# Streamed operand blocks 2080 instead of 2048 bytes apart in a two-layer decoder trunk

## The chip, the cores and the metric

The kernel runs on one core of a Trainium2 chip. The metric is the device time of one execution in microseconds. Three runs of the kernel before gave 2125.79, 2126.0 and 2127.0 us, median 2126.0 us. Nothing else runs on the chip.

## The reference

The program is a decoder trunk of two layers over 256 positions with a model width of 2048, all in float32. What matters here is its large products; everything else is small beside them.

```python
D_MODEL = 2048; SEQ = 256; DEPTH = 2; D_FF = 5632
# layer 0: chunked gMLP gating (12 groups x 128) beside 4-head cross-attention into 256 memory tokens
z = h @ w_in_a[l]                                   # 2048 x 3584
# layer 1: latent attention (12 heads) beside the same cross-attention
kv = rmsnorm(x, g_kv) @ w_kv_a;  z = h @ w_in_b[j]  # 2048 x 576, 2048 x 1024
...
kv = rmsnorm(mem, g_mem) @ w_mem_kv                 # 2048 x 1024, each layer
x = x + jnp.concatenate([main, mo], axis=-1) @ w_out[l]               # 2048 x 2048, each layer
x = x + conv_ffn(rmsnorm(x, g_ffn[l]), w_ffn_up[l], ..., w_ffn_down[l])  # 2048 x 11264, 5632 x 2048
```

The output is a final RMSNorm of x, 256 x 2048.

## The kernel before, in words

**Operands.** TensorE multiplies in the format float32r, which keeps fewer bits than float32, so every large product is made of three: high part by high part, low part by high part, high part by low part. An activation operand is a tile of 16 blocks; block k holds the 128 features k*128 to k*128+127 on the partitions, and along the partition 256 positions of the high part and then 256 of the low part, 512 columns or 2048 bytes in all. There are four such big operands: `xhl` (the normalized stream), `memhl` (the memory tokens), `mainhl` (what w_out multiplies) and `h` (the hidden units of the ffn). The last three share one place in SBUF (tag "big"); `xhl` has its own (tag "xhl"), and in layer B the plain tile `scratch` takes that place. The smaller operands `qhl` and `chl` of layer B have the same 2048-byte blocks, in a pool of their own.

**Weights.** `chunk` (L92 to L125) loads two k-blocks of 512 columns, 512 KB, by one DMA from SP's queue into `raw` (L98), ScalarE rounds them into `whi` (L117), and VectorE writes the remainder to `wlo` (L118; with a gain L122 and L123). Each of the three has four buffers of 4096 bytes on a partition, and `schedule_with_timeline_sim` lets a planner set the order of the instructions on each engine.

**Feature-major products.** `gemm_fm` (L158) takes two chunks at a time, that is four k-blocks by up to four output blocks. Inside a chunk the loop goes over output blocks, and innermost over the two k-blocks, so consecutive matmuls stream block k, block k+1, block k, block k+1 and so on of the same pair. `mm_fm` (L135) makes two bursts of them: `high` (L140) streams all 512 columns of a block against `whi`, `low` (L144) streams the first 256 against `wlo` and adds into the second half of the accumulator. The two bursts change places from one pair of chunks to the next, so that two bursts of one kind follow each other. Each matmul has its own load of a 128 x 128 weight block (LDWEIGHTS, shown as PEld).

**Token-major products.** `gemm_tm` (L187) turns the roles round: `mm_tm` (L179) streams 512 columns of `whi` (L182), `wlo` (L183) and `whi` again (L184), and the weight that is loaded into the array is a 128-column piece of the operand. It serves the values of the memory attention, the first projection of layer A, the values of layer B and the down-projection of the second ffn.

**Writers of the operands.** `put_mem` (L436) writes two blocks of `memhl` by one ScalarE and one VectorE instruction; `split` and `split_gain` (L227 to L235) write one block at a time. `new_hl` (L532) makes a new `xhl` tile for each product that writes one, and `ffn` (L558) one `h` tile for each of its three parts.

The weights of a chunk begin at multiples of 512 bytes within the 4096-byte buffers, and the blocks of the operands at multiples of 2048 bytes within their tiles.

Of the kernel before, what the change touches and what calls it, by code (L numbers as in the profile page):

```python
# [8 lines left out]
F32 = mybir.dt.float32  # L9
F32R = mybir.dt.float32r  # L10
# [3 lines left out]
ALU = mybir.AluOpType  # L14
AX = mybir.AxisListType

P = 128
D = 2048
S = 256
NB = D // P  # L20
# [10 lines left out]
THETA = 10000.0  # L31
EPS = 1e-6
FF_GROUPS = (4, 4, 3)


def exact_pieces(value, bits, count):
# [30 lines left out]
    return out  # L67


class Kernel:  # L70
    def __init__(self, ctx, tc, t, out):
        self.tc, self.nc, self.t, self.out = tc, tc.nc, t, out
# [11 lines left out]

    def psum(self, dt=F32):
        return self.ps.tile([P, 512], dt, tag="ps", name=self.uid("ps"))

    def tmp(self, pool, shape, tag, bufs=2, dt=F32):
        return pool.tile(shape, dt, tag=tag, name=self.uid(tag), bufs=bufs)
# [330 lines left out]
    def start(self):  # L420
        nc, t, tc = self.nc, self.t, self.tc
        self.x = self.ap.tile([P, NB, S], F32, name="xT")
        self.xhl = self.ap.tile([P, NB, 512], F32R, tag="xhl", name=self.uid("xhl"))
        mhl = self.ap.tile([P, NB, 512], F32R, tag="big", name=self.uid("memhl"))
        self.kT = [pool.tile([P, MH, S], F32, name=self.uid("kT")) for pool in (self.mk, self.cp)]
        self.mv = [pool.tile([P, 2, MW], F32, name=self.uid("mv")) for pool in (self.mk, self.cp)]
        self.rt = self.cp.tile([P, 2], F32, name="rt0")
        self.rb = self.tmp(self.cp, [P, S], "rbc", 2)
        with tc.tile_pool(name="st", bufs=1) as st:
            self.gp = st  # L430
            mtok = [st.tile([P, D], F32, name=f"mtok{tb}") for tb in range(2)]
            xtok = [st.tile([P, D], F32, name=f"xtok{tb}") for tb in range(2)]
            mrt = st.tile([P, 2], F32, name="mrt")
            mrb = st.tile([P, S], F32, name="mrb")

            def put_mem(k, acc):  # L436
                a = acc.rearrange("p (k s) -> p k s", k=2)
                hi = mhl[:, k : k + 2, :S]
                nc.scalar.activation(hi, a, AF.Copy)
                nc.vector.tensor_tensor(mhl[:, k : k + 2, S:], a, hi.bitcast(F32), ALU.subtract)  # L440

            def put_x(k, acc):
                for i in range(2):
                    self.split_gain(self.xhl[:, k + i, :], acc[:, i * S : (i + 1) * S], self.gain("g_mix", k + i))
                nc.scalar.activation(self.x[:, k : k + 2, :], acc.rearrange("p (k s) -> p k s", k=2), AF.Copy)

            def mem_piece(h):
                return lambda: (self.token_load(t["mem"][0], mtok, h), self.token_transpose(mtok, h, put_mem))

            load = lambda h: lambda: self.token_load(t["x"][0], xtok, h)  # L450
            trans = lambda h: lambda: self.token_transpose(xtok, h, put_x)
            self.token_load(t["mem"][0], mtok, 0)
            self.gains(("g_mem",))
            self.token_transpose(mtok, 0, put_mem)
            hooks = [
                {
                    0: [mem_piece(1)], 2: [mem_piece(2)], 4: [mem_piece(3)],
                    5: [lambda: self.token_rstd(mtok, st, mrt), lambda: self.gains(("g_mix", "g_ffn", "g_kv"))],
                    6: [self.masks],
                    7: [lambda: self.spread(mrb, mrt)],  # L460
                },
                {
                    0: [load(0), load(1)], 1: [load(2), load(3)], 3: [trans(0)], 5: [trans(1)],
                    6: [lambda: self.gains(("g_v", "g_kv_lat", "g_q_lat"))],
                },
                {0: [trans(2)], 2: [trans(3)], 4: [lambda: self.token_rstd(xtok, st, self.rt)]},
                {1: [lambda: self.spread(self.rb, self.rt)], 2: [lambda: self.conv_consts(0)], 4: [lambda: self.conv_consts(1)]},
            ]
            for l in range(2):
                w = t["w_mem_kv"][l]  # L470
                kT, v = self.kT[l], self.mv[l]

                def ek(b, acc):
                    nc.gpsimd.tensor_tensor(kT[:, b, :], self.join(acc), mrb, ALU.mult)

                def ev(tb, acc):
                    nc.scalar.activation(v[:, tb, :], acc, AF.Copy, scale=mrt[:, tb : tb + 1])

                m = lambda k: mhl[:, k, :]
                g = lambda k: self.gain("g_mem", l * NB + k)  # L480
                self.gemm_fm(self.rows(w, 0, MW), list(range(NB)), MH, m, ek, gain=g, hooks=hooks[2 * l])
                self.gemm_tm(self.rows(w, MW, MW), NB, MW, m, ev, gain=g, hooks=hooks[2 * l + 1])
# [47 lines left out]
        nc.vector.tensor_tensor(x[:, j, :], acc[:, S:], x[:, j, :], ALU.add)  # L530

    def new_hl(self):  # L532
        self.xhl = self.ap.tile([P, NB, 512], F32R, tag="xhl", name=self.uid("xhl"))
        self.ssum = self.tmp(self.cp, [P, S], "ssum", 2)

    def next_operand(self, j, gain):
# [21 lines left out]
    def ffn(self, l, after=None, to_tokens=None, tokens=None):  # L558
        nc, t = self.nc, self.t
        rb = self.tmp(self.cp, [P, S], "rbc", 2)  # L560
        xhl, ssum = self.xhl, self.ssum
        first = {1: [lambda: self.rstd_bc(rb, ssum, D)]}
        up, down = t["w_ffn_up"][l], t["w_ffn_down"][l]
        with self.tc.tile_pool(name=self.uid("ff"), bufs=1) as fp:
            g0 = 0
            for part, ng in enumerate(FF_GROUPS):
                h = self.ap.tile([P, NB, 512], F32R, tag="big", name=self.uid("h"))

                def conv(b, acc):
                    a = self.tmp(fp, [P, S], "a", 2)  # L570
                    nc.gpsimd.tensor_tensor(a, self.join(acc), rb, ALU.mult)  # L571
                    c = self.tmp(fp, [P, S], "c", 3)
                    w = lambda j: self.cT[:, l, j, b : b + 1]
                    nc.scalar.activation(c, a, AF.Identity, scale=w(2), bias=w(3))  # L574
                    nc.vector.scalar_tensor_tensor(c[:, 1:], a[:, : S - 1], w(1), c[:, 1:], ALU.mult, ALU.add)  # L575
                    nc.vector.scalar_tensor_tensor(c[:, 2:], a[:, : S - 2], w(0), c[:, 2:], ALU.mult, ALU.add)  # L576
                    return c

                for g in range(g0, g0 + ng):
                    gate = self.tmp(fp, [P, 4, S], "gate", 2)  # L580

                    def eg(b, acc):
                        c = conv(4 * g + b, acc)
                        nc.scalar.activation(gate[:, b, :], c, AF.Silu)

                    def ev(b, acc):
                        c = conv(FB + 4 * g + b, acc)
                        hv = self.tmp(fp, [P, S], "hv", 2)
                        nc.vector.tensor_tensor(hv, gate[:, b, :], c, ALU.mult)
                        self.split(h[:, 4 * (g - g0) + b, :], hv)  # L590

                    ks = list(range(NB))
                    turns = to_tokens if to_tokens is not None and g == 1 else {}
                    self.gemm_fm(self.rows(up, g * 512, 512), ks, 4, lambda k: xhl[:, k, :], eg, hooks=first if g == 0 else {})
                    self.gemm_fm(self.rows(up, FF + g * 512, 512), ks, 4, lambda k: xhl[:, k, :], ev, hooks=turns)
                last = part == len(FF_GROUPS) - 1
                if last and l == 0:
                    self.new_hl()
                dn = down[g0 * 512 : (g0 + ng) * 512]
                for j in range(4):  # L600
                    src = self.rows(dn, j * 512, 512)
                    if tokens is not None:
                        self.gemm_tm(
                            src, 4 * ng, 512, lambda k: h[:, k, :], lambda tb, acc: tokens(j, tb, acc, last), late=3 if last and j == 3 else 0
                        )
                        continue

                    def ed(b, acc):
                        self.add_residual(4 * j + b, acc)
                        if last:  # L610
                            after(4 * j + b)

                    self.gemm_fm(src, list(range(4 * ng)), 4, lambda k: h[:, k, :], ed)
                g0 += ng


    def layer_a(self):
        nc, t, tc = self.nc, self.t, self.tc
# [3 lines left out]
        with ExitStack() as ctx:  # L622
# [51 lines left out]
            hooks = {1: [spatial_weights], **{4 + i: [lambda i=i: gates(3 * i)] for i in range(4)}}  # L674
            self.gemm_fm(self.rows(w, 2 * GW, MW), ks, MH, x, eq, hooks=hooks)

            hl = self.ap.tile([P, NB, 512], F32R, tag="big", name=self.uid("mainhl"))
            p = {}

            def scores(h):  # L680
# [31 lines left out]
    def layer_b(self):  # L712
# [9 lines left out]
        with tc.tile_pool(name="lb", bufs=1) as lb:  # L722
# [49 lines left out]
            hooks = {2: [lambda: rotate(krT, kr)], 5: [lambda: fq(qhl, QR, "g_q_lat")]}  # L772
            self.gemm_fm(self.rows(w, QR, MW), ks, MH, x, em, gain=gm, hooks=hooks)

            hl = self.ap.tile([P, NB, 512], F32R, tag="big", name=self.uid("mainhl"))
            scratch = self.ap.tile([P, NB * 512], F32, tag="xhl", name="scratch")
            v = scratch[:, : 2 * GW].rearrange("p (a c) -> p a c", a=2)
            wuv = t["w_uv"][0].rearrange("r h v -> r (h v)")

# [221 lines left out]
```

## Time and profile before

| | before |
|---|---|
| median of three runs | 2126.0 us |
| span of the profiled execution, first to last instruction | 2125.1 us |
| PE busy | 2101.5 us, 99% of the span |
| PEld busy | 1831.1 us, 86% |
| VectorE busy | 1465.7 us, 69% |
| ScalarE busy | 1148.7 us, 54% |
| GpSimd busy | 392.8 us, 18% |
| mean granted TensorE clock | 0.998 |
| moved from and to HBM | 392.01 MB, 184 GB/s over the span |

The span leaves out what lies around the first and last instruction, which is why the runs, at 2125.79 us and up, stand a little above it. A busy time of PE counts a matmul from its start to its modelled end, and consecutive matmuls overlap: a burst is best read from the start of its first matmul to the start of what follows, divided by the number of matmuls. That quotient is called the pace below.

### The profile page before, as it was taken

To read this page: it belongs to the slowest core of one execution; us is meant where nothing else is said; L and a number is where in the kernel's file an instruction comes from. 1 tells how busy PE (TensorE), PEld (TensorE's weight loads), DVE (VectorE), ACT (ScalarE), POOL (GpSimd) and SP (SyncE) were. 2 spreads that over 40 slices of the span, in tenths; PEclk is the share of its full clock that TensorE was granted. 3 is DMA by queue.
4 is the path that set the end of the run, shared out by engine and by line. 5 is a ranking of instruction groups with operands and counts; after the bars stand their busy time and mean duration, and the time that the engine had idled before them with its cause. 6 is when DMAs were issued, how large, how long until landed. Compare 5 with 4: busy or idle time off the path is not lost.

```text
span 2125.1 us, 31077 instructions
## 1 busy us (share of the span) xinstructions
PE 2101.5 (99%) x11624; PEld 1831.1 (86%) x11624; DVE 1465.7 (69%) x2186; ACT 1148.7 (54%) x1773; POOL 392.8 (18%) x378
## 2 busy tenths in 40 slices
PE   8999999999999999999999999999999999999998
PEld 7888888888888888888888788888888888888886
DVE  6655667777756777567798766677775577745775
ACT  7654654556535555356556554466553555535554
POOL 1000123312101121011254111332120121201210
PEclk9999999999999999999999999999999999999999
DMA  8565555666566665666655533665656666656664
GB/s 272 178 202 178 159 187 189 189 189 191 189 194 187 185 195 188 197 182 188 192 181 165 171 114 110 196 190 170 191 196 195 187 190 190 194 195 188 189 188 149
DMA packets 207548, 392.01 MB, mean 184 GB/s; under 512 B 14302, under 2 KB 22820, under 8 KB 207268
## 3 DMA queue, kind: packets, MB, share of 16 engines
q1 hardware_dynamic: 207252, 389.50, 59.3%
q8 instruction: 91, 1.49, 0.3%
q14 instruction: 61, 0.50, 0.1%
q10 hardware_dynamic: 144, 0.52, 0.1%
HBM read 387.88 MB, written 2.10 MB: 184 GB/s over the span
## 4 chain that ended last, share of the span: by engine, by line
PE 97%; DVE 1%; ACT 1%; DMA 1%; issue 0%; SPq 0%; DVEq 0%; ACTq 0%
PE ps L140 50%; PE ps L144 26%; PE ps L182 6%; PE ps L184 6%; PE ps L183 6%; PE ps L831 1%; DMA raw<-in_w_mem_kv 0%; PE ps L829 0%; PE ps L523 0%; PE ps L488 0%; DVE wlo L118 0%; PE ps L665 0%; PE ps L852 0%; DMA raw<-in_w_in_a 0%; PE ps L393 0%
## 5 line engine op out<-in xcount | busy, mean ns | idle before, releaser
L118 DVE TENSOR_TENSOR wlo<-raw,whi 128x1024 fp32r<-128x1024 f32 x660 | 843.1, 1288 | 490.3 <-ACT whi L117 362.4
L117 ACT ACTIVATE whi<-raw 128x1024 fp32r<-128x1024 f32 x660 | 697.2, 1058 | 702.7 <-PE ps L140 525.4
L140 PE MATMUL ps<-xhl,whi 128*128 128x512 f32 x3280 | 768.9, 390 | 0.0
L140 PEld LDWEIGHTS ps<-xhl,whi 128*128 128x128 f32 x3280 | 608.6, 188 | 121.7
L571 POOL TENSOR_TENSOR a<-js,rbc 128x256 f32<-128x256 f32 x176 | 230.5, 1323 | 1101.7 <-DVE js L224 1005.8
L144 PEld LDWEIGHTS ps<-xhl,wlo 128*128 128x128 f32 x3280 | 408.7, 192 | 9.2 <-DVE wlo L118 0.6
L144 PE MATMUL ps<-xhl,wlo 128*128 128x256 f32 x3280 | 413.4, 283 | 0.4 <-DVE wlo L118 0.4
L140 PE MATMUL ps<-h,whi 128*128 128x512 f32 x704 | 164.8, 390 | 0.0
L574 ACT ACTIVATE c<-a,cT 128x256 f32<-128x256 f32 x176 | 105.2, 598 | 96.9 <-POOL a L571 95.3
L140 PEld LDWEIGHTS ps<-h,whi 128*128 128x128 f32 x704 | 130.6, 188 | 26.0
L183 PE MATMUL ps<-wlo,h 128*128 128x512 f32 x352 | 136.8, 389 | 0.0
L182 PE MATMUL ps<-whi,h 128*128 128x512 f32 x352 | 136.6, 389 | 0.0
L184 PE MATMUL ps<-whi,h 128*128 128x512 f32 x352 | 136.3, 389 | 0.0
L140 PE MATMUL ps<-mainhl,whi 128*128 128x512 f32 x512 | 119.7, 390 | 0.0
L140 PEld LDWEIGHTS ps<-mainhl,whi 128*128 128x128 f32 x512 | 95.1, 188 | 19.1
L123 DVE SCALAR_TENSOR_TENSOR wlo<-raw,gT,whi 128x512 fp32r<-128x512 f32 x112 | 87.9, 829 | 25.2 <-ACT whi L122 23.0
L576 DVE SCALAR_TENSOR_TENSOR c<-a,cT,c 128x254 f32<-128x254 f32 x176 | 101.1, 587 | 0.0
L575 DVE SCALAR_TENSOR_TENSOR c<-a,cT,c 128x255 f32<-128x255 f32 x176 | 91.6, 539 | 11.6 <-ACT c L574 11.4
L122 ACT ACTIVATE whi<-raw,gT 128x512 fp32r<-128x512 f32 x112 | 74.7, 716 | 42.3 <-PE ps L140 20.0
L224 DVE TENSOR_TENSOR js<-ps,cr 128x256 f32<-128x256 f32 x213 | 84.1, 417 | 12.6 <-POOL a L571 12.3
L222 ACT ACTIVATE cr<-ps 128x256 f32<-128x256 f32 x243 | 79.4, 373 | 19.7 <-PE ps L140 16.5
L144 PEld LDWEIGHTS ps<-h,wlo 128*128 128x128 f32 x704 | 87.7, 191 | 2.0
(248 smaller groups left out, 1856.2 us busy)
## 6 DMA issues: line engine op xcount, KB each, us to landing
raw<-in_w_ffn_up SPq DMA_DIRECT2D x352, 512.0 KB, 4.2
raw<-in_w_ffn_down SPq DMA_DIRECT2D x176, 512.0 KB, 4.4
raw<-in_w_out SPq DMA_DIRECT2D x64, 512.0 KB, 4.1
raw<-in_w_in_a SPq DMA_DIRECT2D x56, 512.0 KB, 4.1
raw<-in_w_mem_kv SPq DMA_DIRECT2D x32, 512.0 KB, 4.8
raw<-in_w_in_b SPq DMA_DIRECT2D x16, 512.0 KB, 3.9
raw<-in_w_uq SPq DMA_DIRECT2D x12, 384.0 KB, 3.3
raw<-in_w_kv_a SPq DMA_DIRECT2D x8, 512.0 KB, 4.2
```

Of the source, the lines that this page charges most:

```text
L117: nc.scalar.activation(hi[:, :n], raw[:, :n], AF.Copy)
L118: nc.vector.tensor_tensor(lo[:, :n], raw[:, :n], hi[:, :n].bitcast(F32), ALU.subtract)
L123: nc.vector.scalar_tensor_tensor(lo[:, s], raw[:, s], gains[k], hi[:, s].bitcast(F32), ALU.mult, ALU.subtract)
L140: mm(acc[:, :], wh, x, start=first, stop=last)
L144: mm(acc[:, S:], wl, x[:, :S], start=False, stop=False)
L182: mm(acc, xh, wh, start=first, stop=False)
L183: mm(acc, xh, wl, start=False, stop=False)
L184: mm(acc, xl, wh, start=False, stop=last)
L571: nc.gpsimd.tensor_tensor(a, self.join(acc), rb, ALU.mult)
L574: nc.scalar.activation(c, a, AF.Identity, scale=w(2), bias=w(3))
L575: nc.vector.scalar_tensor_tensor(c[:, 1:], a[:, : S - 1], w(1), c[:, 1:], ALU.mult, ALU.add)
L576: nc.vector.scalar_tensor_tensor(c[:, 2:], a[:, : S - 2], w(0), c[:, 2:], ALU.mult, ALU.add)
```

## The change

The four big operands get another layout. A tile has eight pairs of blocks, a pair takes 4352 bytes instead of 4096, and the second block of a pair begins 2080 bytes behind the first (PITCH, 520 columns) instead of 2048. The first block of each pair begins at a multiple of 4352 bytes. A small class `Blocks` gives the same indexing as before; `put_mem` takes the two blocks of a pair through `pair`. Since the two places in SBUF are 34816 bytes on a partition instead of 32768, 4096 bytes more in all, the scratch space that the program sets aside for GpSimd's own DMAs is cut to 4096. The number, shape and data of all instructions stay as they are written in the program. `qhl`, `chl`, `raw`, `whi` and `wlo` keep their layout.

```diff
+PITCH = 512 + 8
+PAIR = 1024 + 64
...
+class Blocks:
+    def __init__(self, t):
+        self.t = t
+
+    def pair(self, k):
+        return self.t[:, k // 2, : 2 * PITCH].rearrange("p (i c) -> p i c", i=2)
+
+    def __getitem__(self, at):
+        _, k, cols = at
+        return self.pair(k)[:, k % 2, :512][:, cols]
...
+    def blocks(self, tag, name):
+        return Blocks(self.ap.tile([P, NB // 2, PAIR], F32R, tag=tag, name=self.uid(name)))
...
-        self.xhl = self.ap.tile([P, NB, 512], F32R, tag="xhl", name=self.uid("xhl"))
-        mhl = self.ap.tile([P, NB, 512], F32R, tag="big", name=self.uid("memhl"))
+        self.xhl = self.blocks("xhl", "xhl")
+        mhl = self.blocks("big", "memhl")
...
-                hi = mhl[:, k : k + 2, :S]
+                hi, lo = mhl.pair(k)[:, :, :S], mhl.pair(k)[:, :, S:512]
                 nc.scalar.activation(hi, a, AF.Copy)
-                nc.vector.tensor_tensor(mhl[:, k : k + 2, S:], a, hi.bitcast(F32), ALU.subtract)
+                nc.vector.tensor_tensor(lo, a, hi.bitcast(F32), ALU.subtract)
...
-                h = self.ap.tile([P, NB, 512], F32R, tag="big", name=self.uid("h"))
+                h = self.blocks("big", "h")
...
-            scratch = self.ap.tile([P, NB * 512], F32, tag="xhl", name="scratch")
+            scratch = self.ap.tile([P, NB // 2 * PAIR], F32, tag="xhl", name="scratch")
...
-    nc = bacc.Bacc("TRN2", target_bir_lowering=False, num_devices=1)
+    nc = bacc.Bacc("TRN2", target_bir_lowering=False, num_devices=1, dynamic_dma_scratch_size=4096)
```

`new_hl` and both `mainhl` tiles are changed in the same way as `xhl` and `h`.

More of the change, by code (lines that the diff above doesn't have):

```diff
@@ L532, in new_hl @@
     def new_hl(self):
-        self.xhl = self.ap.tile([P, NB, 512], F32R, tag="xhl", name=self.uid("xhl"))
+        self.xhl = self.blocks("xhl", "xhl")
         self.ssum = self.tmp(self.cp, [P, S], "ssum", 2)
@@ L675, in layer_a @@
             self.gemm_fm(self.rows(w, 2 * GW, MW), ks, MH, x, eq, hooks=hooks)
-            hl = self.ap.tile([P, NB, 512], F32R, tag="big", name=self.uid("mainhl"))
+            hl = self.blocks("big", "mainhl")
             p = {}
@@ L773, in layer_b @@
             self.gemm_fm(self.rows(w, QR, MW), ks, MH, x, em, gain=gm, hooks=hooks)
-            hl = self.ap.tile([P, NB, 512], F32R, tag="big", name=self.uid("mainhl"))
-            scratch = self.ap.tile([P, NB * 512], F32, tag="xhl", name="scratch")
+            hl = self.blocks("big", "mainhl")
+            scratch = self.ap.tile([P, NB // 2 * PAIR], F32, tag="xhl", name="scratch")
             v = scratch[:, : 2 * GW].rearrange("p (a c) -> p a c", a=2)
```

## The prediction

> **What bounds the kernel now.** First the page: the busy shares, the chain of work that ended last, and the clock from the view of the cores.
>
> ```profile
> span 2125.1 us, 31077 instructions
> PE 2101.5 (99%) x11624; PEld 1831.1 (86%) x11624; DVE 1465.7 (69%) x2186; ACT 1148.7 (54%) x1773; POOL 392.8 (18%) x378
> PE 97%; DVE 1%; ACT 1%; DMA 1%; issue 0%; SPq 0%; DVEq 0%; ACTq 0%
> core 0: 2125.1 us, clock 0.998
> ```
>
> PE is the bound over the whole span: 97% of the chain is PE, only 23.6 us of the span find it idle, and the clock is granted in full. A faster kernel must shorten matmuls or the gaps between their starts. So the next view is the timeline of PE in the second half of the first ffn: start, merged length, and count.
>
> ```profile
> 1000.22 7.44 PE L140 MATMUL ps<-xhl,whi 128*128 128x512 f32 x32
> 1007.50 4.00 PE L144 MATMUL ps<-xhl,wlo 128*128 128x256 f32 x32
> 1011.33 7.44 PE L140 MATMUL ps<-xhl,whi 128*128 128x512 f32 x32
> ```
>
> From start to start 32 high matmuls take 7.28 us, 227.5 ns each, and 32 low ones 3.83 us, 119.7 ns each. The settled pace of 512 columns is seen more finely in the token-major stage (the first and the last of seven rows of that view):
>
> ```profile
> 1840.73 0.39 PE L183 MATMUL ps<-wlo,h 128*128 128x512 f32 x1
> ...
> 1842.09 0.39 PE L183 MATMUL ps<-wlo,h 128*128 128x512 f32 x1
> ```
>
> Six matmuls in 1.36 us, 226.7 ns. With 120 ns for 256 columns, 256 further columns cost 106.7 ns, 0.417 ns a column. So 512 columns are worth 213.3 ns, 256 are worth 106.7, and each matmul has a **fixed part of 13.3 ns** besides, the same for both lengths. That part is the only thing that a layout can touch: the number of columns does not change.
>
> How much of it there is follows from the groups by line and shape:
>
> ```profile
> L140 PE MATMUL ps<-xhl,whi 128*128 128x512 f32 x3280 | 768.9, 390 | 0.0
> L144 PE MATMUL ps<-xhl,wlo 128*128 128x256 f32 x3280 | 413.4, 283 | 0.4 <-DVE wlo L118 0.4
> L140 PE MATMUL ps<-h,whi 128*128 128x512 f32 x704 | 164.8, 390 | 0.0
> L182 PE MATMUL ps<-whi,h 128*128 128x512 f32 x352 | 136.6, 389 | 0.0
> L140 PE MATMUL ps<-mainhl,whi 128*128 128x512 f32 x512 | 119.7, 390 | 0.0
> L182 PE MATMUL ps<-whi,xhl 128*128 128x512 f32 x96 | 37.6, 391 | 0.0
> L140 PE MATMUL ps<-memhl,whi 128*128 128x512 f32 x128 | 32.9, 410 | 3.5 <-DVE memhl L440 2.5 <-ACT whi L122 1.0
> L182 PE MATMUL ps<-whi,memhl 128*128 128x512 f32 x64 | 25.4, 400 | 0.0
> ```
>
> 3280 + 704 + 512 + 128 = 4624 high matmuls stream a block of a big operand, and as many low ones, since mm_fm makes one of each per job: 9248. Another 3 x (352 + 96 + 64) = 1536 have a big operand as the loaded weight and stream a weight buffer, whose layout stays. The fixed part of the 9248 is 123 us of the span, 5.8%.
>
> **Is the fixed part inherent?** Two rows speak against a constant. In the timeline these are float32 matmuls, whose columns take two passes' worth of time:
>
> ```profile
> 49.26 1.03 PE L393 MATMUL ps<-ident,xtok 128*128 128x128 f32 x8
> L393 PE MATMUL ps<-ident,xtok x32: 270/272/273, 49.3 to 75.1; 128*128 128x128 f32 x32
> ```
>
> Eight of them last 1.03 us, one 0.272, so the pace is 758 / 7 = 108.3 ns, each with its own weight load as well. If a column costs twice 0.417 ns there, 106.7 ns are columns and the fixed part is 1.6 ns; that the column is exactly twice as dear is my reading, not a row. And the fixed part depends on history. In the chain, in order of time, bursts of two lengths:
>
> ```profile
> 767.00 7.28 PE ps L140 x32
> 1044.84 9.09 PE ps L140 x40
> ```
>
> The eight further matmuls cost 1.81 us, 226.3 ns each, so the first ones of a burst take more than the rest, about 0.03 us in all. Behind a break the settled pace also comes late:
>
> ```profile
> 1207.26 0.40 PE L183 MATMUL ps<-wlo,chl 128*128 128x512 f32 x1
> ...
> 1209.11 0.39 PE L182 MATMUL ps<-whi,chl 128*128 128x512 f32 x1
> ```
>
> Eight matmuls in 1.85 us, 231.3 ns, with the same shapes and the same kind of addresses as the stage with 226.7. A constant of the format would not do that. Something that two streams share, and that depends on how they meet, would: while a block streams, the weights of the next matmul are being read (PEld is busy 86% of the span). If the shared thing is chosen by address, the layout matters; if only by time, it does not. The trace can't tell: the weights of a burst begin at eight places 512 bytes apart, the operands at multiples of 2048 bytes, and in those steps nothing changes the pace. Steps of 32 bytes, the ones that the change makes, occur nowhere in these products.
>
> The page "TensorE: Matmul & The Clock Gate" of the Trainium skill, section "Wait — 56ns, not 53.3ns?", gives about 2.5 ns as the fixed cost of a warm matmul; the 13.3 ns here are five times that, and an estimate by that page is that 10.8 ns of each are avoidable, 100 us over the 9248.
>
> **The change, part by part.**
>
> *Second block of a pair 32 bytes on.* It adds and removes no instruction; it acts on the fixed part alone. Bounds for one matmul: at best the part falls from 13.3 ns to the 1.6 of the transposes, 11.7 x 9248 = 108 us less. On the other side it rises to what the unsettled row shows, 231.3 - 226.7 = 4.6 ns more on the 4624 high ones, 21 us more; a low burst has nothing to lose by such a row. I take the value about halfway from the settled row to the floor, a fixed part of 6.7 ns: only every other block is moved, so at each step one of the two streams still begins where it did, and a halved cost is nearer to the settled row than the floor is. 6.7 x 9248 = **61.7 us less**.
>
> *Pairs 4352 bytes apart.* A pair begins 256 bytes further against the grid of 2048 than the one before. Within a burst this matters once, between its two chunks: nothing, or one matmul's worth (at most 4.6 ns) at some 290 places (9248 / 32), under 1.4 us either way.
>
> *The operand as a loaded weight.* 1536 token-major matmuls load it from places 32 bytes shifted and stream whi and wlo as before. Bounds: 1536 x 11.7 = 18 us less, 1536 x 4.6 = 7 us more. I take nothing, since three in a row load from one block and the unchanged stream is the four times longer read.
>
> *Writers.* ScalarE and VectorE write as many elements; put_mem keeps one instruction for two blocks. The rows below carry the larger work of the same two engines; a write of a block is off PE's chain as long as they have this idle time. What an edit of theirs could cost is bounded by PE's one wait of 2.5 us on memhl above.
>
> ```profile
> L118 DVE TENSOR_TENSOR wlo<-raw,whi 128x1024 fp32r<-128x1024 f32 x660 | 843.1, 1288 | 490.3 <-ACT whi L117 362.4
> L117 ACT ACTIVATE whi<-raw 128x1024 fp32r<-128x1024 f32 x660 | 697.2, 1058 | 702.7 <-PE ps L140 525.4
> ```
>
> *Scratch cut.* The DMA queues of the page:
>
> ```profile
> q1 hardware_dynamic: 207252, 389.50, 59.3%
> q8 instruction: 91, 1.49, 0.3%
> q14 instruction: 61, 0.50, 0.1%
> q10 hardware_dynamic: 144, 0.52, 0.1%
> ```
>
> Hardware queues and instruction fetches only, and no issue comes from GpSimd: nothing waits for that space, cost nothing.
>
> *What is late next.* A chunk is eight high and eight low matmuls, 2.77 us now and 2.67 at the forecast, 2.59 at the floor. ScalarE needs 1.06 us of that for whi and VectorE 1.29 for wlo; ScalarE's idle time in front of whi ends mostly on PE, which frees the buffers. A DMA brings 512 KB per chunk; at 2.59 us that is 202 GB/s, and the first slice of this row shows 272:
>
> ```profile
> GB/s 272 178 202 178 159 187 189 189 189 191 189 194 187 185 195 188 197 182 188 192 181 165 171 114 110 196 190 170 191 196 195 187 190 190 194 195 188 189 188 149
> ```
>
> So no other engine takes over. *Sum*: span 2125.1 - 61.7 = 2063.4, and with the 0.9 us by which the median of the runs, 2126.0, stands over the span, **2064 us**, 2.9% faster.
>
> **The rivals.**
>
> *R1, the shift unsettles the streams (slower).* For it: the settled pace is reached only after some matmuls, and each block begins 32 bytes to the other side of the last one, so it may never be reached. Price: 4.6 ns on each of 4624 high matmuls, 21 us, **2147 us**. It decides from the point where the mean pace of a high burst in the ffn stands over 227.5 ns without the low one gaining as much. Against it: low bursts begin their settled pace at once, and the unsettled row is from another stage.
>
> *R2, the address has no part in it (same).* The fixed part stays 13.3 ns whatever the layout, **2126 us**. For it: the pace is the same whatever operand, buffer and weight column is read, and whether the stream is an operand or a weight. Against it: only that no row has a step under 512 bytes. The page "SBUF — State Buffer" of the Trainium skill, section "Who interferes with whom", says that PE has two independent read ports and never waits on anyone, by which this case holds; the 231.3 ns against 226.7 for like matmuls fit badly with it.
>
> *R3, the fixed part goes almost whole.* Down to the 1.6 to 2.5 ns of other matmuls: 100 to 108 us, with the loaded operands up to 18 more, **2018 us** (108 us). It needs that a shift of every second block suffices.
>
> *R4, only the low bursts gain.* In a low burst the stream and the weight load are of one length, so they meet throughout; in a high one the load is over by half. 6.7 x 4624 = 31 us, **2095 us**.
>
> That the order of instructions changes, because the planner sees other access patterns, is part of each: PE is idle for 23.6 us in all, which caps what that could bring, and I give it 2 us either way.
>
> **How the numbers follow.** Forecast (2040 to 2085) 0.30; R4 or an equally small gain (2085 to 2121) 0.18; R3 (2005 to 2040) 0.14; R2 0.15; R1 0.23. A measurement of this kernel can tell about 0.2%, 4 us, from no change. Faster by more: 0.30 + 0.18 + 0.14 = 0.62; within: 0.15; slower: 0.23. The time given is the forecast's, 2064. The range takes in R3's working down to 2015, the same case and R1 up to 2148. What is left out is a larger loss and a gain that takes the loaded operands along, together under 2 in 10.
>
> **What would show it.** In the changed profile: the starts of an x32 high burst in the ffn 7.07 us apart instead of 7.28 (221 ns each), of a low one 3.63 instead of 3.83 (113 ns): forecast. 7.28 and 3.83 again: R2. High bursts of 7.4 us: R1. Only the low bursts shorter: R4. The token-major stage should keep its 226.7 ns and the counts of matmuls stay; chl and qhl, which are not moved, are the control. A longer wait of PE on whi, wlo or a DMA than the few microseconds of now would contradict the step on what is late next. The prediction is wrong if the fixed part is chosen by time alone, or if the 32 bytes are the wrong step for what is shared.

## The result

The changed kernel takes 2137.38 us (median of four runs, 2137.35 to 2137.92) against 2126.03 us of the kernel before in the same session: a ratio of 1.005, 95% interval 1.0035 to 1.0064. It is 11 us **slower**. The forecast was 62 us faster.

The page of the changed kernel, the busy shares, the chain, and the line of the clock:

```profile
span 2135.6 us, 31077 instructions
PE 2111.8 (99%) x11624; PEld 1824.0 (85%) x11624; DVE 1466.4 (69%) x2186; ACT 1149.3 (54%) x1773; POOL 392.3 (18%) x378
...
PEclk9999999999999999999999999999999999999999
...
PE 97%; ACT 1%; DVE 1%; DMA 0%; issue 0%; SPq 0%; ACTq 0%
```

PE is still the whole chain, its idle time is what it was (23.8 us against 23.6), the clock is full (0.998), and every engine has as many instructions as before. So the 10.5 us of span are in the matmuls. The timeline of PE in the first ffn (start, merged length, count; L157 is the high burst, L161 the low one):

```profile
1000.95 3.95 PE L161 MATMUL ps<-xhl,wlo 128*128 128x256 f32 x32
1004.74 7.52 PE L157 MATMUL ps<-xhl,whi 128*128 128x512 f32 x32
1012.10 3.95 PE L161 MATMUL ps<-xhl,wlo 128*128 128x256 f32 x32
1015.88 7.52 PE L157 MATMUL ps<-xhl,whi 128*128 128x512 f32 x32
```

From start to start a high burst takes 7.36 us, 230.0 ns a matmul (7.28 and 227.5 before), a low one 3.79, 118.4 ns (3.83 and 119.7). High lost 2.5 ns, low gained 1.3. And the token-major stage, which the forecast left alone, in the same view (the first and the last of sixteen consecutive matmuls):

```profile
1844.97 0.40 PE L199 MATMUL ps<-whi,h 128*128 128x512 f32 x1
...
1848.45 0.39 PE L199 MATMUL ps<-whi,h 128*128 128x512 f32 x1
```

Fifteen steps in 3.48 us are 232 ns, where there were 226.7; over the whole trace the stage's three parts have means of 231.1, 231.1 and 231.4. Summed over all matmuls of a kind, from each start to the next, the two traces differ like this:

| us, from each start to the next | before | after | difference |
|---|---|---|---|
| 4624 high matmuls on a big operand | 1056.7 | 1067.6 | +10.9 |
| 4624 low ones | 555.0 | 548.7 | -6.3 |
| 1536 token-major ones that load a big operand | 349.4 | 356.0 | +6.6 |
| all other 840 | 149.6 | 148.4 | -1.2 |

The sum, +10.0 us, is the change of the span to within half a microsecond. The operands that were not moved, `qhl` and `chl`, keep their paces in both traces: 231 and 229 ns high, 119.6 and 118.6 low.

### The profile page after: what moved, and what is told of

It is laid out like the page before. It is cut to its first block, busy times and chain, and to the rows that moved or that the text cites. A ratio compares the mean times of both kernels' runs of the same rounds, so it can differ in the third digit from the quotient of the medians.

```text
span 2135.6 us, 31077 instructions
## 1 busy us (share of the span) xinstructions
PE 2111.8 (99%) x11624; PEld 1824.0 (85%) x11624; DVE 1466.4 (69%) x2186; ACT 1149.3 (54%) x1773; POOL 392.3 (18%) x378
## 4 chain that ended last, share of the span: by engine, by line
PE 97%; ACT 1%; DVE 1%; DMA 0%; issue 0%; SPq 0%; ACTq 0%
PE ps L157 51%; PE ps L161 26%; PE ps L201 6%; PE ps L200 6%; PE ps L199 6%; PE ps L848 1%; PE ps L846 0%; PE ps L540 0%; PE ps L505 0%; PE ps L410 0%; ACT junk L422 0%; PE ps L682 0%; PE ps L869 0%; DMA graw<-in_g_mem 0%; DMA raw<-in_w_in_a 0%
## 5 line engine op out<-in xcount | busy, mean ns | idle before, releaser
L157 PE MATMUL ps<-xhl,whi 128*128 128x512 f32 x3280 | 776.7, 393 | 0.0
L157 PEld LDWEIGHTS ps<-xhl,whi 128*128 128x128 f32 x3280 | 608.2, 188 | 128.9
L161 PEld LDWEIGHTS ps<-xhl,wlo 128*128 128x128 f32 x3280 | 404.2, 188 | 9.9 <-DVE wlo L135 0.6
L161 PE MATMUL ps<-xhl,wlo 128*128 128x256 f32 x3280 | 408.8, 281 | 0.4 <-DVE wlo L135 0.4
L157 PE MATMUL ps<-h,whi 128*128 128x512 f32 x704 | 166.5, 392 | 0.0
L157 PEld LDWEIGHTS ps<-h,whi 128*128 128x128 f32 x704 | 130.4, 188 | 27.7
L157 PE MATMUL ps<-mainhl,whi 128*128 128x512 f32 x512 | 120.9, 393 | 0.0
L157 PEld LDWEIGHTS ps<-mainhl,whi 128*128 128x128 f32 x512 | 95.0, 188 | 20.3
L140 DVE SCALAR_TENSOR_TENSOR wlo<-raw,gT,whi 128x512 fp32r<-128x512 f32 x112 | 87.9, 828 | 25.6 <-ACT whi L139 23.1
L161 PEld LDWEIGHTS ps<-h,wlo 128*128 128x128 f32 x704 | 86.8, 188 | 2.1
```

The source lines that it names most:

```text
L140: nc.vector.scalar_tensor_tensor(lo[:, s], raw[:, s], gains[k], hi[:, s].bitcast(F32), ALU.mult, ALU.subtract)
L157: mm(acc[:, :], wh, x, start=first, stop=last)
L161: mm(acc[:, S:], wl, x[:, :S], start=False, stop=False)
```

## The experiments

The pace of a stage below is the mean from start to start of its consecutive matmuls in the trace, without the steps in which PE waited or did something else; it is good to about 0.1 ns. "High" and "low" stand for high and low matmuls. The question was what the 32 bytes act on. Three theories: **W**, the distance between the streamed block and the weights that are loaded meanwhile; **S**, the step from one streamed block to the next; **P**, the padding of the pairs. For the layouts, `Blocks` got a list of byte offsets, and each tile an entry of a table, by its name and number or `all`; the changed kernel would be `grid(0, 2080, 4352)` for all. The cuts below show the entries, several to a line:

```diff
+def grid(base=0, pitch=2048, pair=4096):
+    return [base + k // 2 * pair + k % 2 * pitch for k in range(16)]
```

**The pairs' padding alone**:

```diff
+    'all': grid(0, 2048, 4352),
```

> One part of the change alone: pairs 4352 bytes apart, the second block 2048 bytes behind the first. Theory W (the pace depends on where a streamed block begins against the weights that are read meanwhile, in steps under 256 bytes): as before, 2126 us, high bursts at 227 ns a matmul, low at 120, token-major at 227. Theory S (the pace depends on the step between two blocks that follow each other): also 2126 us, since that step is 2048 bytes within a pair. Theory P (the padding of the pairs does it): as the changed kernel, 2137 us, high 230, low 118, token-major 231.

2126.9 us against 2126.78, ratio 1.0 (0.999 to 1.0009); 227.5 high, 119.8 low, 226.7 token-major in the ffn stages, all as before. P falls.

**The second block's place alone**:

```diff
+    'all': grid(0, 2080, 4608),
```

> The other part alone: the second block 2080 bytes behind the first, pairs 4608 bytes apart, so each pair begins at a multiple of 512 bytes. Theories W and S: as the changed kernel, 2137 us, high bursts 230 ns a matmul, low 118, token-major 231. Theory P: 2126 us with 227, 120 and 227.

2137.77 us, ratio 1.0055 (1.0038 to 1.0072), with 230.0, 118.4 and 231.1 ns. This is the whole change; it leaves W and S.

**All blocks 32 bytes on, no alternation**:

```diff
+    'all': grid(32, 2048, 4096),
```

> All blocks of the four operands begin 32 bytes later against the weight buffers; blocks 2048 bytes apart as before, so no alternation. Theory S: as before, 2126 us and 227, 120, 227 ns. Theory W: not as before, another pace for every block, high or low, at least 2 ns off in one of the two kinds of burst. A third possibility, that only the alternation unsettles the streams: 2126 us as well.

2149.35 us, ratio 1.0107 (1.0092 to 1.0122): twice the loss. The chain in order of time (start, length, matmuls; L169 high, L173 low):

```profile
1010.65 7.47 PE ps L169 x32
1018.12 3.74 PE ps L173 x32
1021.86 7.46 PE ps L169 x32
```

High goes to 233.3 ns (7.465 / 32), low to 117, and the token-major stage to 233.3 as well. Every block is now where every second one is in the changed kernel, the step from block to block is 2048 bytes again, and the loss has doubled. S falls, and so does the third possibility, that only the alternation unsettles something. The changed kernel's 230.0 lies halfway between 226.7 and 233.3.

**Other distances of the operand**, one for each tile, so that one run gives many:

```diff
+    'xhl1': grid(16), 'memhl1': grid(32), 'mainhl1': grid(16), 'xhl2': grid(32),
+    'h1': grid(64), 'h2': grid(128), 'h3': grid(256), 'xhl3': grid(96), 'mainhl2': grid(192), 'xhl4': grid(48),
...
```

> Blocks 2048 bytes apart, but each operand tile begins at another distance from the grid of the weights: first xhl 16 bytes, memhl 32, first mainhl 16, second xhl (the one of the first ffn) 32, the three h of the first ffn 64, 128 and 256, third xhl (layer B) 96, second mainhl 192, fourth xhl (second ffn) 48, the h of the second ffn 64, 128, 256. Read by stage from the starts of matmuls. Theory S: every stage at 227, 120 and 227 ns. Theory W: the paces differ from stage to stage, with the distance, and repeat at some multiple; at least one distance lies under the 227 or the 120 of before.

2144.59 us in one run. 256 bytes repeat 0 (h3: 228.0 and 119.6 ns, before 227.9 and 119.5); at 64 bytes 229.0 and 116.1; 128 gave 233.4 and 118.5; 16 gave 231.7 and 116.7. The second `mainhl`, 192 bytes on, has low bursts that no stage of before has (L182 high, L186 low):

```profile
1316.89 3.63 PE ps L186 x32
1320.53 7.46 PE ps L182 x32
1327.99 3.63 PE ps L186 x32
```

3.63 us are 113.5 ns, with high at 233. By the prediction's 106.7 ns for 256 columns that is a fixed part of 6.8 ns in place of 13.3. As theory W expected, the paces differ with the distance and a distance beats the 120 of before.

**Other distances of the second block**:

```diff
+    'xhl2': grid(0, 2112, 4608), 'h1': grid(0, 2176, 4608), 'h2': grid(0, 2304, 4608),
+    'xhl3': grid(0, 2144, 4608), 'mainhl2': grid(0, 2240, 4608), 'xhl4': grid(0, 2056, 4608),
...
```

> Pairs at multiples of 512 bytes, the second block at another distance behind the first: first xhl 2064, memhl 2112, first mainhl 2064, second xhl (first ffn) 2112, h of the first ffn 2176, 2304, 2560, third xhl 2144, second mainhl 2240, fourth xhl 2056, h of the second ffn 2064, 2112, 2304. Theory W with each block for itself: a stage runs at the mean of the paces of its two places, as 230.0 is the mean of 226.7 and 233.3 in the changed kernel: 2112 bytes (0 and 64) 228.2 high and 118.0 low, 2176 (0 and 128) 230.4 and 119.2, 2304 and 2560 as before, 227.5 and 119.8, 2144 (0 and 96) 230.3 and 119.9, 2240 (0 and 192) 230.3 and 116.7. If the alternation has an effect of its own, these miss by over 1 ns.

2145.87 us in one run. 2304 and 2560 bytes are as before (227.7 and 119.8; 228.1 and 119.6), 2144 gives 230.2 and 119.9 as expected, 2176 229.9 and 118.2. But 2112 gives 231.3 and 119.0, not 228.2 and 118.0; 2240 gives 227.4, not 230.3; and 2056 234.7 and 119.9. So the rule of the mean, by which each block counts for itself, holds for some steps only. That the changed kernel hits it is not proof of it: its high matmuls start 230 ns apart one after another, not 227 and 233 by turns.

**More distances of the operand**:

```diff
+    'memhl1': grid(80), 'xhl1': grid(112), 'mainhl1': grid(144), 'xhl2': grid(160),
+    'h1': grid(176), 'h2': grid(208), 'h3': grid(224), 'xhl3': grid(240), 'mainhl2': grid(8), 'xhl4': grid(200),
...
```

> As the first sweep, other distances from the grid of the weights: memhl 80 bytes, first xhl 112, first mainhl 144, second xhl (first ffn) 160, h of the first ffn 176, 208, 224, third xhl 240, second mainhl 8, fourth xhl (second ffn) 200, h of the second ffn 192, 96, 224. Theory W with a grid of 256 bytes: high bursts between the 227 of 0 and the 234 of 32 and 128, low ones between 113 and 120, with the lowest low pace near 192; no distance beats both 227 and 120 by more than the 64 bytes of the first sweep did (229 and 116).

2156.08 us in one run. High lies from 230.5 to 234.5 ns everywhere in these stages, low from 116.6 to 120.0; 200 bytes give 120.0, beside the 113.5 of 192. High at 208 and 240 (234.5 and 233.8) is a little over the expected ceiling of 234 or at it, and low has no valley around 192, only that one place. The two were read in different stages.

**The weights in place of the operand.** Operands as before, `wlo` of the feature-major products 64 bytes later:

```diff
-        lo = self.wp.tile([P, 1024], F32R, tag="wlo", ...)
+        lo = self.wp.tile([P, 1024 + 64], F32R, tag="wlo", ...)[:, shift // 4 : shift // 4 + 1024]
...
-                hi, lo = self.chunk(src(kbs[c], nk), nk, nblk * P, g)
+                hi, lo = self.chunk(src(kbs[c], nk), nk, nblk * P, g, shift=64)
```

> The operands lie as in the kernel before; the wlo buffers of the feature-major products alone begin 64 bytes later (token-major ones as before, scratch cut as in the changed kernel). In the sweep an operand 192 bytes past the grid had low bursts at 113.5 ns and high ones at 233; 256 bytes was like none. Theory W, relative: an operand 192 bytes behind the weights is one 64 bytes before them, so the low bursts come to 113.5 ns, the high ones stay at 227.5: 6.3 ns on 4624 matmuls, 29 us less, 2097 us. If the absolute place of the operand counts and not that of the weights: 119.8 and 227.5 ns, 2126 us.

2117.1 us, ratio 0.9952 (0.9935 to 0.9969). Moving the weights changes the pace, as W says, and it gains 10 us; but low stands at 117.8, not at the 113.5 that the mirrored distance had. High stays at 227.5. So the distance to its own weights alone does not give the pace of a low burst.

**Operands and weights together**, 160 bytes further:

```diff
+        self.pad = cp.tile([P, 40], F32, name="pad")
+        nc.vector.memset(self.pad, 0.0)
         self.ident = cp.tile([P, P], F32, name="ident")
```

> Operands and weights are moved by 160 bytes together (a 160-byte tile ahead of everything), their distance as before. If only their difference counts: 2126 us, 227.5 high, 119.8 low, 226.7 token-major. If each one's own place on the 256-byte grid counts: other paces, by 1 ns or more in a kind of burst.

2126.59 us; 227.5, 119.8 and 226.7 ns, stage by stage equal to before within 0.2 ns. The chain in order of time, with the lines of the kernel before (L140 high, L144 low):

```profile
1000.32 7.28 PE ps L140 x32
1007.60 3.83 PE ps L144 x32
```

At this distance the place itself does not count. It is the one joint move that was tried.

**44 distances of the weights in one run**, one for each call in the up-projections, whi and wlo alike. A call is one use of `gemm_fm`, 64 high and 64 low matmuls here; a pair in the table gives the bytes by which whi and wlo begin later:

```diff
+SHIFTS = (
+    [(0, 0), (16, 16), (32, 32), ... (336, 336)],
+    [(352, 352), ... (496, 496), (8, 8), (24, 24), ... (68, 68)],
+)
...
-..., hooks=turns)
+..., hooks=turns, shift=SHIFTS[l][2 * g + 1])
```

> The operands lie as before. In the two up-projections each of the 22 calls of the feature-major product has its whi and wlo chunks at another distance from the grid: first ffn 0, 16, 32 ... 336 bytes in order, second ffn 352 ... 496, then 8, 24, 40, 56, 72, 88, 104, 120, 184, 200, 4, 68. If only the difference between stream and weights counts, on a grid of 256 bytes, a shift s of the weights gives the paces that the operand sweeps gave for 256 - s: 192 as the operand's 64 (229 high, 116 low), 224 as 32 (233, 117), 64 as 192 (233, 113.5), and 256 + s repeats s. The run with wlo 64 bytes later gave 117.8 and not 113.5, against that: if the places count for themselves, the paces don't mirror.

2133.82 us in one run. Ten of the distances:

| whi and wlo later by, bytes | high ns | low ns | 256 more: high, low |
|---|---|---|---|
| 0 | 227.8 | 119.8 | 227.6, 119.8 |
| 16 | 226.7 | 118.3 | 226.7, 118.3 |
| 32 | 233.2 | 118.6 | 233.2, 118.6 |
| 64 | 233.2 | 115.7 | 233.3, 115.7 |
| 88 | 233.1 | 114.0 | |
| 96 | 234.2 | 117.4 | 234.2, 117.4 |
| 120 | 226.8 | 119.1 | |
| 160 | 233.6 | 119.9 | 233.6, 119.9 |
| 192 | 230.5 | 117.8 | 230.4, 117.8 |
| 240 | 228.2 | 117.3 | 227.8, 117.3 |

Sixteen distances come a second time 256 bytes further, hundreds of microseconds later. Fourteen of them repeat within 0.4 ns, most of these within 0.1. Two do not: 144 bytes gave 231.8 high and 118.1 low and then 233.2 and 119.9, and 128 gave 232.5 high and then 233.4. The paces do not mirror the operand sweeps: 192 gives 230.5 and 117.8, while the operand at 64 gave 229.0 and 116.1. One call of it, both at 16 bytes, in the chain (L144 high, L148 low):

```profile
396.52 3.79 PE ps L148 x32
400.30 7.25 PE ps L144 x32
407.56 3.79 PE ps L148 x32
```

7.25 us for 32: 226.7 ns from the first matmul on.

**Combinations**:

```diff
+    [(16, 0), (16, 8), (16, 16), ... (16, 168)],
+    [(16, 176), ... (16, 248), (16, 84), ... (0, 88), (0, 8), (120, 88), ... (240, 88), (0, 4)],
```

> Operands as before; whi 16 bytes later in nearly all of the 44 up-projection calls (the distance at which the high bursts stood at 226.7 from their first matmul), wlo at 0, 8, 16 ... 248 in order, then 84, 92, 76, 4; the last eight calls take other whi: (0, 88), (0, 8), (120, 88), (120, 8), (120, 64), (120, 216), (240, 88), (0, 4). If each kind of burst depends on its own distance alone, high stays at 226.7 for whi 16 throughout, and low repeats the first sweep of the weights: 118.3 at 16, 116.0 at 8, 115.7 at 64, 114.0 at 88, 118.6 at 128. If a burst's pace hangs on the state in which the other one left the streams, as 117.8 against 115.7 for 64 bytes suggests, low differs by over 1 ns from these at several distances, and high is not 226.7 everywhere.

2132.49 us in one run. Its third call has both at 16 bytes, the same layout as the rows above:

```profile
419.93 3.79 PE ps L148 x32
423.72 7.46 PE ps L144 x32
431.18 3.78 PE ps L148 x32
```

High is at 233 ns here, at 226.7 there. The buffers have the same sizes in both kernels, so the operands lie at the same places, and the shapes are equal; what differs is the call ahead, (16, 8) here and (0, 0) there. The accumulators differ too, since a call takes four of the eight. But in the kernel before, calls in turn take other accumulators as well, and the pace stays at 227.5. So **one distance allows more than one lasting pace**. That the state in which the bursts are entered chooses is likely and not shown; each of the two paces was read in a single run. With whi at 16 nearly all calls stood at 230 to 233, only (16, 240) at 226.9. Low moved as well: 115.3 ns for (16, 88) and 117.8 for (16, 64), where the first sweep had 114.0 and 115.7 with whi moved as far as wlo. That may be why neither mirror images nor means could be relied on, and every pace of the sweeps was read behind one neighbour only. The calls (0, 88), (240, 88) and (120, 88) were the best: 227.5, 227.5 and 227.0 high, each with 114.0 low.

**The best of them in all feature-major products.** wlo 88 bytes later:

```diff
-                hi, lo = self.chunk(src(kbs[c], nk), nk, nblk * P, g)
+                hi, lo = self.chunk(src(kbs[c], nk), nk, nblk * P, g, shift=(0, 88))
```

> The kernel before with the wlo chunks of all feature-major products 88 bytes later, all else in place. By the sweeps, high stays at 227.5 ns and low comes to 114.0 from 119.8: 5.8 ns on 4624 matmuls, 27 us less, 2100 us. If the state left by other stages decides and the pace of the up-projections is not that of w_out or of the down-projection, less of it: low between 114 and 118, 2100 to 2118 us.

2100.57 us, ratio 0.9875 (0.9858 to 0.9891). The edit also makes the whi and wlo buffers 512 bytes longer and cuts the scratch; with both and no shift, the first sweep of the weights had 227.8 and 119.8. The timeline of PE in the first ffn (L140 high, L144 low):

```profile
1004.82 3.81 PE L144 MATMUL ps<-xhl,wlo 128*128 128x256 f32 x32
1008.47 7.44 PE L140 MATMUL ps<-xhl,whi 128*128 128x512 f32 x32
1015.75 3.81 PE L144 MATMUL ps<-xhl,wlo 128*128 128x256 f32 x32
```

Low bursts take 3.65 us, 114.1 ns each, high ones 7.28 as before. Summed over the trace the low matmuls fall from 555.0 to 529.7 us, the high ones stay (1056.7 and 1056.2): 25 of the 26 us by which the span is shorter.

**whi 120 bytes later as well**:

```diff
-nblk * P, g, shift=(0, 88))
+nblk * P, g, shift=(120, 88))
```

> whi 120 and wlo 88 bytes later. By the sweep high 227.0 and low 114.0, 0.5 ns less than with wlo alone on 4624 matmuls, 2 us: 2098 us. If whi at 120 reaches its settled pace only behind some low bursts, as whi at 16 did, high goes to 233 in some stages and the time over 2110 us.

2100.38 us, ratio 0.9871 (0.9856 to 0.9886); high 227.0, low 114.1. The expected 2 us more can't be told from nothing. Both versions beat the kernel before by 1.3%, and the changed one by more; wlo alone is the smaller edit.

## Why the prediction was wrong

*What bounds the kernel*: right. PE was all of it, and no other engine came late: in the groups by line and shape of the kernel with wlo 88 bytes later, PE's idle time ahead of the largest group of low matmuls (after the bar) is 0.5 us, 0.4 of it for wlo, as before:

```profile
L144 PE MATMUL ps<-xhl,wlo 128*128 128x256 f32 x3280 | 395.6, 277 | 0.5 <-DVE wlo L118 0.4
```

*A fixed part of 13.3 ns that depends on how two streams meet*: right that time beyond the columns can be moved by an address, and shown. It changes with the distance between stream and weights, it mostly repeats after 256 bytes, and it did not change when both were moved by 160 bytes. Its size is not shown. The subtraction that gave 13.3 takes it to be the same for 512 and 256 columns; with wlo 88 bytes later high is 227.5 and low 114.0, and the same subtraction would give 0.443 ns a column and a fixed part of 0.5 ns. What stands without it are the paces: 226.7 to 234.7 ns high, 113.5 to 121.5 low. By the prediction's columns these are fixed parts of 13 to 21 ns and of 7 to 15. What the streams share, a bank or a slot, was not shown; the runs only give its period.

*The value for the second block, a fixed part of 6.7 ns, -61.7 us*: **the step that failed.** It took for granted that a shift moves the part towards the floor. For high matmuls the settled row, 226.7 ns, was already the best that any layout of the sweeps gave; 32 bytes is one of the bad places (233.3). In place of 61.7 us less, every second block there costs 10.9 us on the high matmuls and gives back 6.3 on the low ones, 4.6 us more in all. A trace with one distance alone could not tell the sign, and no row stood behind the halving. The floor of 1.6 ns from the transposes was never approached in these products.

*The operand as a loaded weight, taken at nothing*: wrong by +6.6 us, inside its own bounds (18 less to 7 more). The reason given, that the unchanged stream is four times longer, is void: the pace went from 226.7 to 231 ns with only the loaded side moved, every second block of it, and to 233.3 with all blocks moved. Without this term the change would have cost some 4.6 us (10.9 - 6.3), at the edge of what can be told.

*Pairs 4352 bytes apart, writers, scratch*: nothing, as said; the run with the pairs' padding alone has all three and the time of before.

*Rival R1 (slower, 2147)* had the right sign and the right sort of place, too large on the high bursts (4.6 ns for 2.5) and with neither the low nor the token-major term. Its cause is refuted: shifting all blocks alike, with no change of direction from block to block, is worse still. *R2 (same)* falls with the pace at 32 bytes. The page "SBUF — State Buffer" of the Trainium skill, section "Who interferes with whom", from which R2 drew support, gives PE two independent read ports, one for the moving operand and one for the weights. The runs fit badly with that: at like shapes, clock and order of instructions the matmuls took 226.7 or 233.3 ns by the distance of two SBUF operands. That one read waits for the other is a guess, though, and no trace shows it. *R3* did not occur; *R4*, only the low bursts gain, is what the better layout does (-25 us), not this one. That is no proof of its reason, that a weight load is as long as a low stream and half a high one: in the trace before, the loads of `whi` and `wlo` for `xhl` have records of 188 and 192 ns on average, against paces of 227.5 and 119.8.

*The estimate by the page "TensorE: Matmul & The Clock Gate"* of the Trainium skill, section "Wait — 56ns, not 53.3ns?", takes 2.5 ns of fixed cost and so 100 us to be had. It is not refuted as a limit, but no layout tried came near it: by the prediction's columns the least was 6.8 ns, in low bursts alone.

The range, 2015 to 2148, held the time only because R1's price was in it; the forecast's sign and the chances, 0.62 for faster, did not fit. A row with a steady but unexplained overhead says that something can be moved, not that a given move improves it.

## What to carry to other kernels

When every matmul carries the same overhead beyond its columns, try the byte distance between what is streamed and what is loaded as weights: here one such number was worth -1.3% or +1.1%. Sweep it inside one run, one value for each call of the same product, and read the pace by stage from the starts of the matmuls. Then put the best one into the whole kernel, since the same distance can settle at two paces.

## What the runs showed of the hardware

Three things were not expected. The pace of float32r matmuls depends on the distance between the streamed operand and the weights, and in most pairs of distances 256 bytes apart it repeats within 0.1 ns. Even 8 bytes can matter: low bursts stood at 113.5 ns at 192 bytes and at 120.0 at 200, in two stages. It did not change when both lay 160 bytes further (227.5 and 119.8 again). And it seems to have memory: the same layout ran at 226.7 or at 233 ns in the high bursts of a call, behind different calls. What decides between the two was not found, and neither was the cause of the dependence.
